# One decoder step on one core: low-rank steps placed one by one among a dense projection's groups, and a smaller rate of dense work in the second half

## Chip, core and metric

The kernel runs on one core of one Trainium2 chip. The metric is device time in microseconds, lower is better; a run's time is that of one execution of the whole step.

## What is computed

Two layers are applied to a prompt of 1024 tokens and to eight single sample tokens, width 1024, all in f32. Layer 0 is a convolution branch beside sparse attention. Layer 1, which the change touches, is an RWKV-7 mixer:

```python
xsh = x[None] + (x_prev - x)[None] * mu[:, None, None, :]
r, k, v, z = jnp.einsum('nbtd,nde->nbte', xsh[:4], w_rkvz)
w_raw = -jax.nn.softplus(-(w0 + jnp.tanh(xsh[4] @ w1) @ w2)) - 0.5      # "sigma"
decay = jnp.exp(-jnp.exp(w_raw))
a = jax.nn.sigmoid(a0 + (xsh[5] @ a1) @ a2)
...
def step(S, inp):          # one token
    sa = jnp.einsum('bhvk,bhk->bhv', S, kk_t)
    S = S * w_t[:, :, None, :] - sa[..., None] * (kk_t * a_t)[:, :, None, :] + v_t[..., None] * k_t[:, :, None, :]
    return S, jnp.einsum('bhvk,bhk->bhv', S, r_t)
...
out = (y.reshape(B, T, D_C) * jax.nn.silu(z)) @ w_out        # then x = layer_norm(ALPHA * x + out)
```

So there are four dense projections of 1024 x 1024 (r, k, v, z), two low-rank branches (rank 64), the recurrence, and one dense output product with a layer norm.

## The kernel before

The kernel runs layer 0 first and then layer 1 (`phase_d`, from about 1070 us on in the profile). Every f32 product is three passes of 32-bit "round" matmuls: each operand is split into a hi and a lo part, and hi x hi, lo x hi and hi x lo are summed (`mm3`, L1186 to L1188). A weight of 128 x 1024 comes in by DMA on SP's queue (`wsplit`, L1176); its hi part is made by ACT (L113) and its lo part by POOL or DVE (L121). It then feeds 48 matmuls for 512 tokens. The pool "dw" holds two each of the tiles `w`, `wh` and `wl`.

Each projection and branch is a Python generator, and who calls `next` on them in what order sets the order of emission; a scheduler then orders each engine's instructions by a simulated timeline. `xmake` makes a projection's mixed input (ACT L1209 and L1213, DVE L1210). `t_proj` yields twice for each weight (after each half of 256 tokens), evacuating by ACT L1321. `t_sigma` and `t_a` first run `lora_hidden`, then `lora_w2` makes the second matrix as A (hi, above lo's rows) and B, and then ten (sigma) or eight (a) small groups follow: matmuls L1278 and L1279 with L1281 and L1282 behind them, or L1296 and L1297 with L1298. `lora_w2` takes A and B from the names "wh" and "wl" of the same pool, and keeps them for all its groups.

Tokens come in two halves. The first half (`h` = 0, the "early" stage, about 1070 to 1270 us) follows the string `FSEQ`: k with sigma, then r with a, then v. After it come 16 units (`u`), one for each group of 128 tokens and half of the heads, with eight slots each. A slot does one step of the recurrence (`s3`), pieces of the preparation of the next units (`s2`, `joinUT`, `s1`), and then as much dense work from the list `F1` as `RATE` allows: generators yield their cost (1 unless they say otherwise). In units 0 to 5 F1 holds the second half's projections; what is left is run at the start of unit 6. From unit 6 on it holds z and the output products (`t_out`, L1703 to L1705 in `t_last` and L1774 to L1776), and each output reads the pairs of units that are done; `t_out(2)` is appended at unit 13 and `t_last` at unit 15. `t_out` takes two tiles "big" of a pool with two buffers, for the residual rows (L1757). Behind each output stands a layer norm, `ln_out` (ACT L1657, L1661, L1662; DVE L1667; POOL L1668). L1556 (ACT) is at the end of each unit's recurrence: unit ends stand at 1618 (unit 5), 1678, 1740, 1796, 1881, 1921 (unit 10), 1976, 2026 (unit 12), 2080, 2139 and 2175 us (unit 15: the program's tail begins).

Of the kernel before, what the change touches and what calls it, by code (L numbers as in the profile page):

```python
# [9 lines left out]
F32R = mybir.dt.float32r  # L10
# [719 lines left out]
WD = 3  # L730
SU = 1
TL = 1
RATE = 1.2, 1.1
WK1 = 5
SD = 0
CNAT = ('za', 0)
# [363 lines left out]
def phase_d(nc, tc, I, O, G):  # L1100
# [4 lines left out]
    flat = lambda t: t.rearrange("p a b -> p (a b)")  # L1105
    with ExitStack() as es:
        pool = lambda name, bufs, **k: es.enter_context(tc.tile_pool(name=name, bufs=bufs, **({} if k else {"reuse_waits": "tile"}), **k))
        B = (1, 2, 2, 9, 2, 3)
        up = pool("du", B[0])
        late = pool("dl", 1)  # L1110
        bp = pool("dbig", B[4])
# [4 lines left out]
        wp = pool("dw", B[2])  # L1116
# [135 lines left out]
        def lora_w2(nm):  # L1252
            w = flat(wtile())
            nc.sync.dma_start(w[0:64], I[nm + "2"])
            nc.sync.dma_start(w[64:128], I[nm + "2"])
            A = flat(wp.tile([128, 8, 128], F32R, name="wh"))
            nc.scalar.activation(A, w, AF.Copy)
            B = flat(wp.tile([128, 8, 128], F32R, name="wl"))
            nc.vector.tensor_tensor(B[0:64], w[0:64], A[0:64], op=SUB)
            v = flat(wtile())  # L1260
            nc.gpsimd.memset(v[64:128], 0.0)
            nc.sync.dma_start(v[64:65], I[nm + "0"])
            nc.sync.dma_start(v[96:97], I[nm + "0"])
            nc.scalar.activation(B[64:128], v[64:128], AF.Copy)
            nc.vector.tensor_tensor(B[96:97], v[96:97], B[96:97], op=SUB)
            return A, B

        def t_sigma(h):
            H1, H2 = lora_hidden(h, "w1", 4)
            yield  # L1270
            A, B = lora_w2("w")
            toks = [(i * 128, 128) for i in range(4)] + ([(512, NS)] if h else [])
            for ti, (o, r) in enumerate(toks):
                for c in range(2):
                    yield .3
                    p = acc()
                    sl = slice(c * 512, c * 512 + 512)
                    nc.tensor.matmul(p[0:r], lhsT=H1[:, o:o + r], rhs=A[:, sl], start=True, stop=False)  # L1278
                    nc.tensor.matmul(p[0:r], lhsT=H2[:, o:o + r], rhs=B[:, sl], start=False, stop=True)  # L1279
                    dst = otile()[:, 0:512]  # L1280
                    nc.scalar.activation(dst[0:r], p[0:r], AF.Tanh, scale=0.5)  # L1281
                    (nc.vector if "s" in EV else nc.gpsimd).tensor_scalar(dst[0:r], dst[0:r], 0.5, 0.5, op0=MUL, op1=ADD)  # L1282
                    nc.sync.dma_start(SG[4 * h + ti][:, sl] if ti < 4 else scr["sgs"][:, sl], dst[0:r])
            yield
# [19 lines left out]
        def t_proj(h, nm, i):  # L1304
            x = xmake(h, i)
            W = wsplit(I["w_rkvz"][i, 0])
            yield
            for j in range(8):
                wh, wl = W
                og = otile()  # L1310
                for c, g, lo, hi in chunks(h):
                    p = acc()
                    mm3(p[:, 0:hi - lo], wh, wl, x, lo, hi)
                    if c == 0 and j < 7:
                        W = wsplit(I["w_rkvz"][i, j + 1])
                    if nm == "z":
                        nc.scalar.activation(og[:, lo:hi], p[:, 0:hi - lo], AF.Tanh, scale=0.5)
                        nc.vector.scalar_tensor_tensor(og[:, lo:hi], og[:, lo:hi], 1.0, p[:, 0:hi - lo], op0=ADD, op1=MUL)
                        nc.sync.dma_start(SZ[g][:, j, 0:hi - lo], og[:, lo:hi])
                    else:  # L1320
                        nc.scalar.activation(og[:, lo:hi], p[:, 0:hi - lo], AF.Copy)  # L1321
                        if hi > 512:
                            nc.scalar.activation(smp[:, {"r": 0, "k": 1, "v": 2}[nm], j], p[:, 256:264], AF.Copy)
                    if c == 0:
                        yield
                if nm != "z":
                    nc.sync.dma_start(RT[nm, h, j // 4][:, j % 4], og[:, 0:512])
                yield
# [407 lines left out]
        def t_out(g):  # L1736
            n = 264 if g == 2 else 256
            y = xpair()
            for j in range(8):
                y[0].append(xp.tile([128, 264], F32R, name="xh"))  # L1740
                y[1].append(xp.tile([128, 264], F32R, name="xl"))
                og = sp.tile([128, 264], F32, name="og")
                nc.sync.dma_start(og[:, 0:256], YT[g][j // 4][:, j % 4])
                if g == 2:
                    nc.gpsimd.tensor_copy(og[:, 256:264], G.ysn[:, j])
                sz = sp.tile([128, 264], F32, name="xs")
                nc.sync.dma_start(sz[:, 0:256], SZ[g][:, j, 0:256])
                if g == 2:
                    nc.sync.dma_start(sz[:, 256:264], SZ[3][:, j, 256:264])
                nc.vector.scalar_tensor_tensor(sz[:, 0:n], og[:, 0:n], V(j, 4), sz[:, 0:n], op0=ADD, op1=MUL)  # L1750
                split(nc, y[0][j][:, 0:n], y[1][j][:, 0:n], sz[:, 0:n], nc.scalar, nc.vector, scale=0.5)
                if j % 2:
                    yield
            rows = [(0, 128), (128, 128)] + ([(256, NS)] if g == 2 else [])
            h = [bp.tile([128, D], F32, name="big") for _ in range(2)]
            for ti in range(2):
                nc.sync.dma_start(h[ti], scr["x1"][2 * g + ti])  # L1757
            H = [[x[:, 0:512], x[:, 512:]] for x in h]
            if g == 2:
                H.append([one.tile([128, 512], F32, name="xk", bufs=3) for _ in range(2)])  # L1760
                for f in range(2):
                    nc.sync.dma_start(H[2][f][0:NS], scr["x1"][8][0:NS, f * 512:f * 512 + 512])
            st = sp.tile([128, 3, 8], F32, name="st")
            for f in range(2):
                fs = slice(f * 512, f * 512 + 512)
                p = [(ps if ti < 2 else pm).tile([128, 512], F32, name="mm" if ti < 2 else "sm") for ti in range(len(rows))]
                for k2 in range(4):
                    wh, wl = wsplit(I["w_out1"][f, k2])
                    for k in range(2):
                        a, b = (w[:, 4 * k:4 * k + 4].rearrange("p a b -> p (a b)") for w in (wh, wl))  # L1770
                        kk = 2 * k2 + k
                        for ti, (o, r) in enumerate(rows):
                            yh, yl = y[0][kk][:, o:o + r], y[1][kk][:, o:o + r]
                            nc.tensor.matmul(p[ti][0:r], lhsT=yh, rhs=a, start=kk == 0, stop=False)  # L1774
                            nc.tensor.matmul(p[ti][0:r], lhsT=yh, rhs=b, start=False, stop=False)  # L1775
                            nc.tensor.matmul(p[ti][0:r], lhsT=yl, rhs=a, start=False, stop=kk == 7)  # L1776
                    yield
                for ti, (o, r) in enumerate(rows):
                    nc.vector.scalar_tensor_tensor(H[ti][f][0:r], H[ti][f][0:r], ALPHA, p[ti][0:r],
                                                   op0=MUL, op1=ADD, accum_out=st[0:r, ti, f:f + 1])  # L1780
            gb = []
            for i in (1, 3):
                gb.append(flat(wtile()))
                nc.sync.dma_start(gb[-1], I["ln_rows"][i:i + 1].to_broadcast([128, D]))
            parts = [[(h[ti], slice(0, D))] if ti < 2 else [(H[2][f], slice(f * 512, f * 512 + 512)) for f in range(2)]
                     for ti in range(len(rows))]
            ln_out(rows, parts, st, gb, g, [nc.vector if g == 3 and ti else nc.gpsimd for ti in range(len(rows))])
            yield

        def run(gens, cost):  # L1790
            while gens and cost > 0:
                try:
                    cost -= next(gens[0]) or 1.0
                except StopIteration:
                    gens.pop(0)
            return -cost
# [23 lines left out]
        for g in (g1[0], g1[1], g2[0], gj[0]):  # L1820
            for _ in g:
                pass
        F1 = [t_proj(1, "k", 1), t_sigma(1), t_proj(1, "r", 0), t_a(1), t_proj(1, "v", 2)]
        F3 = []
        over = 0.0
        for u, (g, d) in enumerate(units):
            if u == 6:
                run(F1, 1000)
                F1 = [t_proj(0, "z", 3), t_out(0), t_proj(1, "z", 3), t_out(1)]
# [6 lines left out]
            for k in range(8):  # L1836
# [5 lines left out]
                step(g1[u + 2])  # L1842
                over = run(F1, RATE[u >= 6] - over)
                if k in (2, 6) and u < 11:
# [136 lines left out]
```

## Time and profile before

| what | us |
|---|---|
| median of three runs | 2218.49 |
| the three | 2222.84, 2218.19, 2218.49 |
| the profiled execution, its own time | 2221.96 |
| its span in the trace | 2220.2 |
| busy in it: PE, DVE, ACT, POOL | 1849.8, 1494.3, 1156.8, 979.1 |
| mean granted TensorE clock | 0.867 of full speed |

The span runs from the first to the last instruction; the time has 1.8 us more around it. The granted clock is the share of full speed that the chip's throttle allowed TensorE. Waits are named by what ended them: "ACT wh L113 <- PE mm L1187" means that the split on line 113 could begin when the matmuls of line 1187 had read the old tile.

### The profile page before, as it was taken

The page shows a single profiled execution, that of the slowest core. Times are in us where ns is not written, and L with a number is a line of the kernel's source. Part 1 is how long each engine was busy: PE and PEld are TensorE (multiplying, and loading weights), DVE is VectorE, ACT ScalarE, POOL GpSimd, SP SyncE. Part 2 cuts the span into 40 slices and gives each one's busy share as a digit, 9 for nine tenths or more (in the row PEclk, how much of TensorE's full clock was granted, in tenths as well). Part 3 has the DMA queues.
Part 4 walks back from the last instruction along what each step waited for, and adds up shares of the span by engine and source line. Part 5 has one row for each costly group of instructions (what it writes and reads, how often), then busy time and mean ns, then how long its engine had stood idle before and what let it go on. Part 6 is the DMA issues. An engine that isn't in the chain of part 4 may idle for free. (4 is left out here: it accounts for less than half of the span.)

```text
span 2220.2 us, 41377 instructions
## 1 busy us (share of the span) xinstructions
PE 1849.8 (83%) x16026; PEld 1552.5 (70%) x16026; DVE 1494.3 (67%) x2543; ACT 1156.8 (52%) x2361; POOL 979.1 (44%) x784
## 2 busy tenths in 40 slices
PE   5988897668999997898777999899999786987854
PEld 5987896656767785676666987687788665865533
DVE  5998995547788878226363276856747896487553
ACT  3323323544665545357466465847754585465344
POOL 4667666544655545545334212332344444113233
PEclk9998998857999976899887999897799885987967
DMA  6423344521221213636455443433443454353432
GB/s 241 128 84 131 135 143 152 200 71 34 63 62 47 57 34 96 201 118 184 143 183 183 149 115 102 150 114 109 144 145 118 147 148 136 91 143 113 133 111 102
DMA packets 232095, 275.27 MB, mean 124 GB/s; under 512 B 71545, under 2 KB 171569, under 8 KB 227738
## 3 DMA queue, kind: packets, MB, share of 16 engines
q1 hardware_dynamic: 210712, 215.21, 31.8%
q0 software_dynamic: 7616, 41.52, 5.6%
q10 hardware_dynamic: 13570, 15.90, 2.0%
q8 instruction: 126, 2.06, 0.4%
q14 instruction: 71, 0.58, 0.1%
HBM read 212.47 MB, written 64.27 MB: 125 GB/s over the span
## 5 line engine op out<-in xcount | busy, mean ns | idle before, releaser
L121 POOL TENSOR_TENSOR wl<-w,wh 128x1024 fp32r<-128x1024 f32 x81 | 201.5, 2489 | 353.7 <-ACT wh L113 317.9
L1186 PE MATMUL mm<-xh,wh 128*128 128x256 f32 (+1 forms) x1024 | 310.8, 305 | 17.6 <-ACT og L1321 6.6
L1187 PE MATMUL mm<-xl,wh 128*128 128x256 f32 (+1 forms) x1024 | 302.4, 296 | 1.2 <-POOL xl L1214 0.7
L1188 PE MATMUL mm<-xh,wl 128*128 128x256 f32 (+1 forms) x1024 | 300.4, 295 | 3.5 <-POOL wl L121 2.7
L113 ACT ACTIVATE wh<-w 128x1024 fp32r<-128x1024 f32 (+2 forms) x130 | 134.4, 1035 | 191.6 <-DMA w<-in_w_fm 60.9
L1186 PEld LDWEIGHTS mm<-xh,wh 128*128 128x128 f32 x1024 | 204.3, 200 | 30.0 <-ACT og L1321 9.1
L1187 PEld LDWEIGHTS mm<-xl,wh 128*128 128x128 f32 x1024 | 205.8, 201 | 5.7 <-issue 2.7
L1188 PEld LDWEIGHTS mm<-xh,wl 128*128 128x128 f32 x1024 | 204.3, 200 | 6.2 <-POOL wl L121 3.4
L268 DVE SCALAR_TENSOR_TENSOR c<-U,cw,c 128x1024 f32<-128x1024 f32 x120 | 199.1, 1683 | 0.9
L604 POOL TENSOR_TENSOR Pl<-PT,Ph 128x512 fp32r<-128x512 f32 (+1 forms) x102 | 131.9, 1297 | 151.3 <-DVE Ph L603 121.0
L252 POOL TENSOR_TENSOR cbuf<-cbuf 128x256 f32<-128x256 f32 (+2 forms) x72 | 132.8, 1850 | 87.6 <-ACT cbuf L250 83.5
L217 PE MATMUL S<-xh,wh 128*128 128x344 f32 (+1 forms) x432 | 146.6, 339 | 22.8 <-ACT wh L113 20.4
L219 PE MATMUL S<-xh,wl 128*128 128x344 f32 (+1 forms) x432 | 144.8, 335 | 15.6 <-POOL wl L121 12.3
L218 PE MATMUL S<-xl,wh 128*128 128x344 f32 (+1 forms) x432 | 146.4, 339 | 4.1 <-POOL xl L121 3.9
L1214 POOL TENSOR_TENSOR xl<-xs,xh 128x520 fp32r<-128x520 f32 (+1 forms) x76 | 106.0, 1398 | 98.8 <-ACT xh L1213 91.2
L250 ACT ACTIVATE cbuf<-cbuf,wrow 128x256 f32<-128x256 f32 x192 | 79.3, 496 | 120.3 <-DMA cbuf<-in_ccmp,cix 77.3
L1210 DVE SCALAR_TENSOR_TENSOR xs<-xk,mu,xs 128x512 f32<-128x512 f32 x96 | 97.1, 1017 | 56.9 <-ACT xs L1209 55.1
L217 PEld LDWEIGHTS S<-xh,wh 128*128 128x128 f32 (+1 forms) x432 | 84.8, 196 | 25.0 <-ACT wh L113 23.6
L562 DVE TENSOR_REDUCE nm<-S 128x1 f32<-128x640 f32 (+7 forms) x128 | 88.0, 698 | 19.8 <-PE S L558 19.1
L219 PEld LDWEIGHTS S<-xh,wl 128*128 128x128 f32 (+1 forms) x432 | 84.3, 195 | 20.6 <-POOL wl L121 14.4
L1398 PE MATMUL pa<-AM,KBK 64*128 64x128 f32 x512 | 70.5, 327 | 29.3 <-DVE KBK L1376 13.2
L218 PEld LDWEIGHTS S<-xl,wh 128*128 128x128 f32 (+1 forms) x432 | 84.8, 196 | 7.7 <-POOL xl L121 4.8
(610 smaller groups left out, 5396.8 us busy)
## 6 DMA issues: line engine op xcount, KB each, us to landing
w<-in_w_rkvz SPq DMA_DIRECT2D x64, 512.0 KB
w<-in_w_out SPq DMA_DIRECT2D x36, 512.0 KB
w<-in_w_fm SPq DMA_DIRECT2D x25, 512.0 KB
xk<-x1T SPq DMA_DIRECT2D x48, 260.0 KB
xk<-x1T SPq DMA_DIRECT2D x48, 256.0 KB
w<-in_w_out SPq DMA_DIRECT2D x16, 256.0 KB
x<-in_xp SPq DMA_DIRECT2D x8, 512.0 KB
x<-x ACTq DMA_DIRECT2D x8, 512.0 KB
```

The costliest lines, as they stand in the source:

```text
L113: nc.scalar.activation(hi, src, AF.Copy, **({} if scale is None else {"scale": scale}))
L121: e_lo.tensor_tensor(lo, src, hi, op=SUB)
L217: nc.tensor.matmul(dst, lhsT=wh[:, k, 0:n], rhs=xh[:, k, sl], start=k == 0, stop=False)
L218: nc.tensor.matmul(dst, lhsT=wh[:, k, 0:n], rhs=xl[:, k, sl], start=False, stop=False)
L219: nc.tensor.matmul(dst, lhsT=wl[:, k, 0:n], rhs=xh[:, k, sl], start=False, stop=k == 7)
L252: nc.gpsimd.tensor_tensor(bv[:, 0:n], bv[:, 0:n], bv[:, n:2 * n], op=ADD)
L268: e.scalar_tensor_tensor(c[:, i, 0:T], u[:, k:k + T], cwh[:, i, k:k + 1], c[:, i, 0:T], op0=MUL, op1=ADD)
L604: lambda: nc.gpsimd.tensor_tensor(Pl[:, 0:w], PT[:, 0:w], Ph[:, 0:w], op=SUB)]
L1186: nc.tensor.matmul(dst, lhsT=wh[:, k], rhs=xh[k][:, lo:hi], start=k == 0, stop=False)
L1187: nc.tensor.matmul(dst, lhsT=wh[:, k], rhs=xl[k][:, lo:hi], start=False, stop=False)
L1188: nc.tensor.matmul(dst, lhsT=wl[:, k], rhs=xh[k][:, lo:hi], start=False, stop=k == 7)
L1214: (nc.vector if early[0] and k % LD == 0 else nc.gpsimd).tensor_tensor(lo[k][:, 0:n], t[:, 0:n], hi[k][:, 0:n], op=SUB)
```

## The change

There are four edits. The second matrix of a low-rank branch, A and B, is taken from the pool of "big" and no longer from "wh" and "wl". In the second half's list F1 the branches are no longer generators of their own between the projections: a new generator `among` emits sigma's groups one by one between the half-weight groups of r, and a's between those of v; each such pair counts 1.15. The four preparation steps of `t_out` count 0.25 and not 1. From unit six on, `RATE` is 0.9 and no longer 1.1 per slot. The early stage's string is untouched.

```diff
-RATE = 1.2, 1.1
+RATE = 1.2, 0.9
...
-            A = flat(wp.tile([128, 8, 128], F32R, name="wh"))
+            A = flat(bp.tile([128, 8, 128], F32R, name="big"))
             nc.scalar.activation(A, w, AF.Copy)
-            B = flat(wp.tile([128, 8, 128], F32R, name="wl"))
+            B = flat(bp.tile([128, 8, 128], F32R, name="big"))
...
                 if j % 2:
-                    yield
+                    yield .25
...
+        def among(proj, lora):
+            yield next(lora) or 1.5
+            yield next(proj)
+            next(lora)
+            for _ in proj:
+                next(lora, None)
+                yield 1.15
+            for x in lora:
+                yield x
...
-        F1 = [t_proj(1, "k", 1), t_sigma(1), t_proj(1, "r", 0), t_a(1), t_proj(1, "v", 2)]
+        F1 = [t_proj(1, "k", 1), among(t_proj(1, "r", 0), t_sigma(1)), among(t_proj(1, "v", 2), t_a(1))]
```

The first place is ACT in the early stage, r beside a (names end in a running number; `og_10390` and `og_10460` are results of r, `og_10450` and `og_10520` of a, `xs` and `xh` an input being made for later). Before:

```order
L1209 ACTIVATE xs_11755<-xk_11756,omu_9080 128x520
L1321 ACTIVATE og_10460<-mm_10461 128x256
L1209 ACTIVATE xs_11766<-xk_11767,omu_9080 128x520
L1213 ACTIVATE xh_11753<-xs_11755 128x520
L113 ACTIVATE wh_10488<-w_10486 128x1024
L1321 ACTIVATE og_10460<-mm_10493 128x256
L1298 ACTIVATE og_10520<-mm_10521 128x256
```

With the change:

```order
L1321 ACTIVATE og_10390<-mm_10423 128x256
L1298 ACTIVATE og_10450<-mm_10451 128x256
L113 ACTIVATE wh_10488<-w_10486 128x1024
L1209 ACTIVATE xs_10756<-xk_10757,omu_9080 128x512
L1213 ACTIVATE xh_10744<-xs_10746 128x512
L1298 ACTIVATE og_10450<-mm_10455 128x256
L1213 ACTIVATE xh_10754<-xs_10756 128x512
L1321 ACTIVATE og_10460<-mm_10461 128x256
L1209 ACTIVATE xs_10766<-xk_10767,omu_9080 128x512
L1209 ACTIVATE xs_10776<-xk_10777,omu_9080 128x512
L1213 ACTIVATE xh_10764<-xs_10766 128x512
```

The split `wh_10488` of the next r weight stood behind `og_10460<-mm_10461`, the evacuation of the weight in use; it now stands ahead of it and of three input steps. `wh_10558` follows in the same way.

The second place is SP's queue in the early stage, k beside sigma (`w_9651`, `w_9718` and `w_9785` are k's first weights, `xk` pieces of x, `rk00` and `rk01` results of k that are stored, `kt` unit 0's load of them). Before:

```order
L1327 DMA rk00_9103<-og_9552 128x512
L1204 DMA xk_9958<-x1T_0_80 128x512
L1176 DMA w_9651<-in_w_rkvz 128x1024
L1204 DMA xk_9968<-x1T_0_80 128x512
L1176 DMA w_9718<-in_w_rkvz 128x1024
L1327 DMA rk01_9104<-og_9625 128x512
L1095 DMA x1T_1_81<-xt_9007 1024x1x8
L1176 DMA w_9785<-in_w_rkvz 128x1024
L1283 DMA sg0_9119<-og_9688 128x512
L1336 DMA kt_11270<-rk00_9103 128x4x128
```

With the change:

```order
L1327 DMA rk00_9103<-og_9552 128x512
L1263 DMA w_9619<-in_w0 1x1024
L1204 DMA xk_9958<-x1T_0_80 128x512
L1204 DMA xk_9968<-x1T_0_80 128x512
L1327 DMA rk01_9104<-og_9625 128x512
L1095 DMA x1T_1_81<-xt_9007 1024x1x8
L1336 DMA kt_11270<-rk00_9103 128x4x128
L1176 DMA w_9651<-in_w_rkvz 128x1024
L1176 DMA w_9718<-in_w_rkvz 128x1024
L1283 DMA sg0_9119<-og_9688 128x512
L1338 DMA st__11273<-sg0_9119 128x512
L1176 DMA w_9785<-in_w_rkvz 128x1024
```

The two weights stood ahead of the store of `og_9625` and the x1T store; they now stand behind both, and behind unit 0's load `kt`. The two residual loads of `t_out(0)` (L1757) are no longer in this place.

The third place is ACT from the end of unit 15 (L1556) on (`wh` are splits of output weights, `xh` inputs of the last output). Before:

```order
L1556 ACTIVATE sq_22500<-pA_22498 128x512
L1558 ACTIVATE Y_22147<-pA_22498,vec_9084 128x128 x4
L1562 ACT_TABLE_LOAD
L1562 ACTIVATE sq_22500<-pB_22506,eps_gn_66 128x512
L1563 ACT_TABLE_LOAD
L1563 ACTIVATE sq_22500<-sq_22500 128x512
L113 ACTIVATE wh_22389<-w_22387 128x1024
L113 ACTIVATE wh_22534<-w_22532 128x1024
L113 ACTIVATE xh_22174<-xs_22512 128x128
L113 ACTIVATE xh_22175<-xs_22517 128x128
```

With the change:

```order
L1556 ACTIVATE sq_22500<-pA_22498 128x512
L1558 ACTIVATE Y_22147<-pA_22498,vec_9084 128x128 x4
L113 ACTIVATE wh_22382<-w_22380 128x1024
L1562 ACT_TABLE_LOAD
L1562 ACTIVATE sq_22500<-pB_22506,eps_gn_66 128x512
L1563 ACT_TABLE_LOAD
L1563 ACTIVATE sq_22500<-sq_22500 128x512
L113 ACTIVATE wh_22394<-w_22392 128x1024
L113 ACTIVATE xh_22174<-xs_22512 128x128
L113 ACTIVATE xh_22175<-xs_22517 128x128
L113 ACTIVATE wh_22428<-w_22426 128x1024
L113 ACTIVATE xh_22176<-xs_22522 128x128
```

Between L1556 and `wh_22534`, the first weight of the last tile's second part, there was one weight split, and now there are four.

Counted on PE between the unit ends in the two orders, dense matmuls of z and of the outputs (behind unit 12 all are of the outputs):

| | unit 8 | 9 | 10 | 11 | 12 | 13 | 14 | 15 | behind it |
|---|---|---|---|---|---|---|---|---|---|
| before | 90 | 102 | 216 | 144 | 72 | 72 | 72 | 55 | 41 |
| with the change | 120 | 72 | 168 | 168 | 96 | 48 | 144 | 24 | 72 |

## Rows read from the trace of the kernel before

**Rows 1.** Part 1 of the page: busy time, share of the span and instructions of PE; then of PEld, DVE and the others.
```profile
PE 1849.8 (83%) x16026; PEld 1552.5 (70%) x16026; DVE 1494.3 (67%) x2543; ACT 1156.8 (52%) x2361; POOL 979.1 (44%) x784
```

**Rows 2.** Busy time of each engine by stretch: stretch in us from the span's start, its length, then busy us (instructions) of PE, PEld, DVE, ACT and POOL, the granted TensorE clock as a share of full speed, the busy share of the DMA engines and their GB/s. The first two are k beside sigma and r beside a in the early stage, the third the dense v projection there, the rest units 2, 3, 6, 9, 10, 14 and 15, what follows unit 15, and all from the end of unit 12.
```profile
1077.80:1108.20 30.40, 23.89 (x149) 21.94 (x150) 6.46 (x5) 7.93 (x18) 6.85 (x6) 0.83 0.50 166
1166.90:1197.40 30.50, 25.55 (x156) 24.17 (x156) 8.97 (x12) 13.32 (x27) 12.71 (x13) 0.79 0.52 176
1232.00:1263.00 31.00, 31.00 (x266) 31.00 (x265) 5.03 (x6) 10.30 (x20) 7.76 (x4) 1.00 0.44 149
1402.00:1448.00 46.00, 41.33 (x473) 30.53 (x473) 42.22 (x81) 41.26 (x86) 19.16 (x22) 0.81 0.51 155
1448.00:1500.00 52.00, 51.41 (x645) 46.60 (x644) 26.39 (x57) 21.86 (x49) 13.48 (x12) 1.00 0.40 122
1618.00:1678.00 60.00, 60.00 (x719) 53.18 (x718) 25.07 (x42) 32.06 (x64) 21.81 (x17) 1.00 0.41 132
1796.00:1881.00 85.00, 58.42 (x756) 46.24 (x755) 70.09 (x133) 53.73 (x105) 38.54 (x32) 0.70 0.48 148
1881.00:1921.00 40.00, 40.00 (x526) 35.85 (x525) 12.25 (x27) 15.08 (x30) 10.85 (x7) 1.00 0.33 104
2080.00:2139.00 59.00, 37.85 (x516) 25.60 (x514) 36.80 (x75) 25.08 (x54) 20.33 (x10) 0.77 0.21 59
2139.00:2175.00 36.00, 30.30 (x260) 20.75 (x260) 11.81 (x27) 16.98 (x30) 9.52 (x5) 0.81 0.61 199
2175.00:2221.00 46.00, 17.29 (x43) 11.29 (x43) 18.72 (x34) 19.48 (x30) 14.94 (x6) 0.67 0.24 83
2026.00:2221.00 195.00, 126.52 (x1242) 85.51 (x1241) 107.62 (x207) 83.21 (x155) 66.12 (x34) 0.75 0.37 119
```

**Rows 3.** Waits of all engines between 1040 and 1260 us: engine, tile and line that waited, for which, us in total, times, longest.
```profile
POOL wl L121 <- ACT wh L113: 59.0, 10, 9.9
ACT wh L113 <- PE mm L1187: 15.3, 7, 2.3
```

**Rows 4.** Timeline of PE: start, duration (us), line, operation, and in brackets the idle time before it and what ended it. The first seven rows are r beside a, from the last matmul before the first stall to the last of the third weight, with two neighbours (1172.41, 1172.62) behind a stall; the last two are from k beside sigma.
```profile
1162.79 0.38 PE L1297 MATMUL mm<-xl,wl 128*128 128x256 f32 x1
1166.87 0.58 PE L1296 MATMUL mm<-xh,wh 128*128 128x256 f32 x1 [3.70 <-ACT og L1321]
1172.41 0.41 PE L1188 MATMUL mm<-xh,wl 128*128 128x256 f32 x1
1172.62 0.41 PE L1186 MATMUL mm<-xh,wh 128*128 128x256 f32 x1
1178.72 0.39 PE L1296 MATMUL mm<-xh,wh 128*128 128x256 f32 x1 [2.10 <-ACT og L1321]
1188.44 0.39 PE L1296 MATMUL mm<-xh,wh 128*128 128x256 f32 x1 [1.06 <-ACT og L1321]
1197.32 0.28 PE L1297 MATMUL mm<-xl,wl 128*128 128x256 f32 x1
...
1077.82 0.39 PE L1186 MATMUL mm<-xh,wh 128*128 128x256 f32 x1 [1.19 <-ACT wh L113]
1084.59 0.40 PE L1279 MATMUL mm<-wl,xl 128*128 128x512 f32 x1
```

**Rows 5.** The load of the weight that is split at 1165.49: its issue on SP's queue, and on ACT its hi part.
```profile
1160.24 0.33 SPq L1176 DMA_DIRECT2D w<-in_w_rkvz  x1
...
1165.49 1.06 ACT L113 ACTIVATE wh<-w 128x1024 fp32r<-128x1024 f32 x1 [2.41 <-DMA w<-in_w_rkvz]
```

**Rows 6.** k beside sigma: issues on SP's queue (the first two k weights, and unit 0's load of kt), the hi part of the first k weight on ACT, and on DVE the last instruction that reads a buffer that one of those weights takes.
```profile
1072.62 0.33 SPq L1176 DMA_DIRECT2D w<-in_w_rkvz  x1
1074.53 0.33 SPq L1176 DMA_DIRECT2D w<-in_w_rkvz  x1
1080.57 0.58 SPq L1336 DMA_DIRECT2D kt<-rk  x1
...
1076.71 1.06 ACT L113 ACTIVATE wh<-w 128x1024 fp32r<-128x1024 f32 x1 [0.35 <-DMA w<-in_w_rkvz]
...
1073.28 1.22 DVE L1265 TENSOR_TENSOR wl<-w,wl 1x1024 fp32r<-1x1024 f32 x1
```

**Rows 7.** ACT in the last 195 us: the last hi part before, and the first behind, a stretch without any; then three of the last output's. And two neighbouring output matmuls of the tail on PE.
```profile
2093.94 1.06 ACT L113 ACTIVATE wh<-w 128x1024 fp32r<-128x1024 f32 x1 [2.30 <-issue]
2147.22 1.06 ACT L113 ACTIVATE wh<-w 128x1024 fp32r<-128x1024 f32 x1 [0.99 <-DMA w<-in_w_out]
...
2190.41 1.04 ACT L113 ACTIVATE wh<-w 128x1024 fp32r<-128x1024 f32 x1
2194.79 1.04 ACT L113 ACTIVATE wh<-w 128x1024 fp32r<-128x1024 f32 x1
2198.89 1.06 ACT L113 ACTIVATE wh<-w 128x1024 fp32r<-128x1024 f32 x1 [3.07 <-PE pa L1705]
...
2171.92 0.40 PE L1703 MATMUL mm<-wh,xh 128*128 128x512 f32 x1
2172.15 0.40 PE L1704 MATMUL mm<-wl,xh 128*128 128x512 f32 x1
```

**Rows 8.** The layer norm's rows at 2122 us: L1667 on DVE by itself and beside POOL's L1668.
```profile
2121.68 0.81 DVE L1667 TENSOR_SCALAR big<-big,st 128x1024 f32<-128x1024 f32 x1
2122.61 2.86 DVE L1667 TENSOR_SCALAR big<-big,st 128x1024 f32<-128x1024 f32 x1
...
2122.57 2.35 POOL L1668 TENSOR_TENSOR big<-big,w 128x1024 f32<-128x1024 f32 x1 [24.39 <-DVE big L1667]
```

**Rows 9.** Waits of PE between 1800 and 1880 us, the longest: us in total, times, longest.
```profile
PE pA L1523 <- DVE SV L1549: 11.7, 1, 11.7
```

## Prediction, made before the changed kernel ran

> **What bounds the kernel now.** I read the busy shares first: PE works for 83% of the span, more than any other engine [rows 1]. That is an average, so the table of stretches comes next [rows 2]; there the reader is to see three kinds of stretch. In the dense v projection of the early stage (1232 to 1263) PE is busy for all 31.0 us, 266 matmuls, 0.117 us each. In units 6 (1618 to 1678) and 10 (1881 to 1921) PE is also busy throughout. Elsewhere it is not: in the two early stretches where a low-rank branch runs beside a dense projection (1077.8 to 1108.2 and 1166.9 to 1197.4) it is busy for 23.9 of 30.4 and 25.6 of 30.5 us at a granted clock of about 0.8; in units 2, 9 and 14 DVE or a chain of small steps is ahead of it.
>
> The two early stretches are explained by the waits of that stage [rows 3]: POOL's lo part (L121) waited 59.0 us for ACT's hi part (L113), and L113 waited 15.3 us for PE's L1187, the last reader of the old weight. The second low-rank matrix A holds one of the two "wh" buffers for the whole branch, so the next weight can be split only when PE has finished the last. The PE timeline shows what that costs at a weight's start [rows 4]: gaps of 3.70 and 2.10 us, then matmuls 0.21 us apart (1172.41, 1172.62), twice the dense pitch: the clock's lower level, 1.2 instead of 2.4 GHz.
>
> **The change part by part.** Every sum is made against the profiled execution (2221.96 us, 0.16% above the median of the three, 2218.49) and then taken off the median.
>
> *The bp buffers, r with a (early).* A no longer holds a "wh", so a weight is split while its predecessor is in use. From the last matmul before the first stall (1162.79) to the end of the third weight (1197.32) pass 34.5 us [rows 4]. Without the stalls a weight costs 48 x 0.118 = 5.7 us plus a seam of 1.3 us (the gap of 1.19 us at 1077.82, behind which the stretch started at full clock), 7.0 in all; three of them and 12 low-rank matmuls (1.4) are 22.4. The load must come earlier too: w was issued at 1160.24 and its split waited for it until 1165.49 [rows 5]; in the new order ACT has that split ahead of three input steps, not behind a projection's evacuation. **-12.1 us.** Ends: 0 (the stalls only change their cause) and -16 (dense pitch, 3 x 5.7 + 1.4 = 18.5).
>
> *The same, k with sigma (early).* Here the new order costs something first. SP issued the first two k weights at 1072.62 and 1074.53 [rows 6]; they now stand behind the load of kt, which was issued at 1080.57. First matmul before: 1077.82. Now: about 1080.3, plus 4.1 us of transfer (1072.62 to the split's start at 1076.71) and 1.06 of split, 1085.5: 7.7 us later. Queued behind the late weights is nothing that PE needs sooner. The three weights then take 3 x 7.0 = 21.0 in place of 30.4, 9.4 less. **-1.7 us.** Ends: -9.4 (the loads come no later, since their buffers come free by DVE's L1265 at 1074.5) and +7.7 (the stalls stay).
>
> *Units 0 to 5.* k, r, v, sigma and a of the second half are the same work; sigma's ten groups move from unit 2 (DVE 42.2 and ACT 41.3 of 46 us) into unit 3, where PE has 51.4 of 52. That relieves one and loads the other by 20 matmuls of 0.40 = 8.0 us (the last row there) [rows 4]. I price it at **0**, ends -8 and +8. The big buffers that the two matrices now take in units 2 to 5 hold nothing else there: t_out(0), which shares them, needs its two residual tiles, now loaded later, only for its first sum in unit 8.
>
> *RATE 0.9 and 0.25 a preparation step (units 6 to 15).* By cost, z and out are now spread over 54/0.9 = 60 slots instead of 60/1.1 = 54.5. Counted in the two orders, 288 output matmuls stand behind the end of unit 12 on PE where 240 stood. The 48 take 48 x 0.235 = 11.3 us (the pitch of L1703 to L1704) [rows 7]. They leave units 6 to 12, 408 us (1618 to 2026), of which 100 (units 6 and 10) are bound by PE: 11.3 x 100/408 = **-2.8 us** gained. They come to the last 195 us, in which PE is idle for 68, so I let that cover hide them; without that cover they cost 11.3. Ends: -11.3 (all of them were in the way) and +17 (unit 14 pays for its whole 72).
>
> *The sum:* -12.1 - 1.7 + 0 - 2.8 = -16.6: 2205.4 against the profiled run, **2202 us** against the median.
>
> **The rivals.** A measurement of this kernel can tell about 0.2% (4.4 us) from no change.
>
> *The late pile-up (slower).* Unit 14 (2080 to 2139) gets 144 output matmuls instead of 72: 16.9 us more of PE. Behind the last unit 72 matmuls of the last output stand instead of 41, three more weights, whose splits came 4.1 to 4.4 us apart [rows 7]: 7.3 us of PE at least, 12.6 by the splits. That is 24 to 29.5 if none of it is hidden, and given back would be at most what units 13 and 15 lose, 24 and 31 matmuls, 12.9. So 11 to 29.5 late, less the 13.8 early: 2216 to 2234, about 2228 if little is given back. It decides when the recurrence's small matmuls, on which unit 14's steps hang, must queue on PE behind the outputs, and when the stretch behind unit 15 is paced by weights. For it: units 13 and 15 end by their own chains, so less work there need not shorten them, and in the last stretch (2175 to 2221) the splits are spaced out already. Against: unit 14 has PE busy for 37.9 of 59 us [rows 2], 21.1 idle, and from 2093.94 to 2147.22 no output weight was split at all [rows 7]: its room is larger than the 16.9. Its upper end has a second reason: DVE's L1667 took 0.81 us by itself and 2.86 beside POOL's L1668 of 2.35 us [rows 8]; with three layer norm tiles pushed together, 2.05 each is up to 6 us more of the same sign. The Trainium skill ("SBUF — State Buffer", Who interferes with whom) says that VectorE and GpSimd share a port pair that is an exclusive lock; the pair of rows agrees in that DVE's end falls with POOL's, and by it the pile-up would come to the upper end that it has here.
>
> *Unit 9 too (faster still).* It takes 85 us where PE has 58.4 and DVE 70.1 of work [rows 2], with one PE wait of 11.7 us for DVE's SV at L1549 [rows 9]. In the new order it has 72 dense matmuls and not 102. If its steps fall out of each other's way, it comes to between DVE's 70.1 and PE's 58.4: 15 to 27 less, 2175 to 2187, about 2181. Against: this wait is on the recurrence's own chain, which the change leaves alone.
>
> *No gain early.* If PE still pauses at each weight long enough, the lower clock stays: 48 x 0.213 + 1.3 = 11.5 us a weight, three are 34.5, as long as now. Then only the late -2.8 is left: about 2216. For it: the granted clock of 0.79 in that stretch [rows 2], and loads that could pace it (each weight 4.1 us or more after its issue). Against: the 1.19 us gap at 1077.82, after which the matmul took 0.39 and not 0.58 us [rows 4]. The Trainium skill ("TensorE: Matmul & The Clock Gate", Part 1: The HAM clock gate) has the clock follow how busy PE has lately been; by that rule shorter gaps bring the full clock, and the sum would be that of the forecast, while by the row of 1166.87 alone (0.58 us after its gap) it would be this rival.
>
> **How the numbers follow.** Forecast 0.50 (its own range 2192 to 2212: r with a off by 4, the other three terms by 6 together); unit 9 too 0.17; late pile-up 0.20; no gain early 0.13. Faster by over 0.2%: 0.50 + 0.17 + 0.03 of the last = 0.70. Within: 0.10 of the last and 0.02 of the pile-up = 0.12. Slower: 0.18. The range reaches from 2178 (half of unit 9's case lies below) to 2229 (half of the pile-up's case lies above), so some 0.18 is left out.
>
> **What would show it.** Early: no gap above 1.5 us at a weight's start while a runs beside r, three weights in 21 to 24 us, a granted clock near 1.0 there; the first k weight at 1085 rather than 1078. If k starts at 1078 the gain is larger by up to 7.7; if a's stretch keeps its 30 us, the no-gain case holds. Units 6 to 12: 408 us becomes about 405; if unit 9 falls to 70 us or below, its case. Late: from the end of unit 12 to the end about 195 us; 205 or more is the pile-up. The prediction is wrong if the time before unit 0 does not fall by 10 us or more, or if the last stretch grows by as much.

## Result: 1.06% longer, and the profile after

The changed kernel took 2237.59 us (median of four, 2236.02 to 2239.89) where the kernel before, in runs beside it, took 2218.34 (four, 2213.85 to 2222.84): ratio 1.0106, 95% interval 1.0078 to 1.0135. The forecast was 2202 us; the time is above the range's end of 2229 as well. The rival that came nearest is the late pile-up (2216 to 2234).

Part 1 of the page of the changed kernel answers to [rows 1]:

```profile
PE 1861.1 (83%) x16026; PEld 1558.5 (70%) x16026; DVE 1495.5 (67%) x2543; ACT 1148.6 (51%) x2355; POOL 979.1 (44%) x784
```

PE is 11.3 us busier with the same 16026 instructions, and the span is 2234.3 us, 14.1 longer. To see where the time went, I set the two traces on the first projection's first matmul (1004.5 before, 999.2 after: the two runs differ by 5.3 us ahead of any change) and compared the unit ends (start of L1556 on ACT). Negative is earlier with the change:

| end of | early stage and unit 0 | 1 | 2 | 4 | 5 | 6 | 7 | 8 | 9 | 10 | 12 | 13 | 14 | 15 | program |
|---|---|---|---|---|---|---|---|---|---|---|---|---|---|---|---|
| us | -10 | 0 | -2 | -5 | -32 | -9 | 8 | 16 | -4 | 8 | 1 | -5 | -5 | 14 | 19 |

So 10 us are won early and given back in unit 1 (48 us long instead of 38); dense work leaves unit 5 and comes back in units 6 to 8; unit 9 is 20 us shorter; by unit 12 the traces are level, and all of the loss appears behind unit 14. The stretches of the changed kernel, with the columns of [rows 2]: k beside sigma (from k's fifth weight to r's first), r beside a (from r's second weight to v's first), the middle of the latter, units 5, 6 and 7, units 14 and 15, what follows, and all behind unit 12:

```profile
1063.60:1116.40 52.80, 34.83 (x217) 29.73 (x215) 20.86 (x21) 23.88 (x46) 18.48 (x22) 0.81 0.54 170
1124.00:1199.80 75.80, 55.84 (x403) 52.59 (x403) 39.20 (x49) 48.75 (x94) 37.30 (x41) 0.88 0.63 199
1159.00:1189.00 30.00, 21.71 (x169) 20.27 (x167) 13.90 (x18) 18.58 (x37) 17.52 (x17) 0.99 0.70 217
1546.00:1580.00 34.00, 30.42 (x257) 23.37 (x257) 26.91 (x60) 21.09 (x44) 12.02 (x17) 0.65 0.36 92
1580.00:1663.00 83.00, 74.36 (x929) 67.05 (x929) 30.86 (x56) 46.92 (x111) 22.57 (x20) 0.96 0.46 146
1663.00:1743.00 80.00, 68.74 (x771) 58.56 (x770) 61.83 (x104) 36.20 (x74) 32.49 (x29) 0.87 0.40 121
2069.00:2129.00 60.00, 53.54 (x445) 32.43 (x444) 25.43 (x58) 20.63 (x34) 15.75 (x9) 0.88 0.46 149
2129.00:2183.00 54.00, 27.06 (x269) 19.76 (x270) 29.51 (x54) 18.74 (x42) 20.06 (x10) 0.62 0.40 121
2183.00:2234.00 51.00, 23.15 (x67) 14.90 (x65) 19.11 (x35) 23.26 (x34) 20.04 (x8) 0.72 0.30 103
2022.00:2234.00 212.00, 144.65 (x1330) 99.20 (x1328) 110.37 (x222) 88.44 (x166) 71.91 (x40) 0.76 0.38 119
```

The kernel before took 53.8 and 82.7 us for the first two of these (same columns):

```profile
1068.70:1122.50 53.80, 36.50 (x217) 30.68 (x215) 21.20 (x21) 24.88 (x48) 17.73 (x22) 0.80 0.55 178
1131.00:1213.70 82.70, 61.54 (x405) 57.05 (x403) 37.42 (x48) 48.31 (x92) 35.72 (x40) 0.82 0.55 176
```

Behind unit 12 it is 212 us instead of 195. Unit 14 keeps its length with 144 output matmuls (PE 53.5 of 60 us busy, 37.9 of 59 before), so its idle time did take them; unit 15 takes 54 us instead of 36, and what follows 51 instead of 45.

### The profile page after: what moved, and what is told of

The parts are those of the page before. It is cut to its first block, busy times and chain, and to the rows that moved or that the text cites. A ratio compares the mean times of both kernels' runs of the same rounds, so it can differ in the third digit from the quotient of the medians.

```text
span 2234.3 us, 41381 instructions
## 1 busy us (share of the span) xinstructions
PE 1861.1 (83%) x16026; PEld 1558.5 (70%) x16026; DVE 1495.5 (67%) x2543; ACT 1148.6 (51%) x2355; POOL 979.1 (44%) x784
## 5 line engine op out<-in xcount | busy, mean ns | idle before, releaser
L121 POOL TENSOR_TENSOR wl<-w,wh 128x1024 fp32r<-128x1024 f32 x81 | 202.4, 2499 | 345.3 <-ACT wh L113 328.6
L113 ACT ACTIVATE wh<-w 128x1024 fp32r<-128x1024 f32 (+2 forms) x130 | 134.5, 1035 | 206.9 <-PE mm L1187 59.1
L121 DVE TENSOR_TENSOR wl<-w,wh 128x1024 fp32r<-128x1024 f32 x45 | 57.0, 1266 | 54.6 <-ACT wh L113 54.3
```

Source lines behind the costliest of these rows:

```text
L113: nc.scalar.activation(hi, src, AF.Copy, **({} if scale is None else {"scale": scale}))
L121: e_lo.tensor_tensor(lo, src, hi, op=SUB)
```

## Experiments

Each ratio is to runs of the kernel before on the same chip; the brackets are 95% intervals. Single runs of one kernel spread far: 33 runs of the kernel before, taken side by side, lay between 2195.95 and 2222.30 us. So terms of 5 us are barely resolved even by a dozen runs.

### The parts of the change, one by one

`e1_early_big`: A and B in big in the early stage alone.

```diff
-            A = flat(wp.tile([128, 8, 128], F32R, name="wh"))
+            A = flat((bp if early[0] else wp).tile([128, 8, 128], F32R, name="big" if early[0] else "wh"))
...
-            B = flat(wp.tile([128, 8, 128], F32R, name="wl"))
+            B = flat((bp if early[0] else wp).tile([128, 8, 128], F32R, name="big" if early[0] else "wl"))
```

> The kernel before, with A and B of the early stage's two branches alone taken from the pool of big (the second half's stay in wh and wl; F1, yields and RATE as before). Theory L (the buffers gain early, the late rate loses): the early stage ends about 10 us sooner and the end follows, 2208 us. Theory M (the groups among r and v lose it): the same, 2208. Rival N (time won early is lost again in the units whatever else is changed): 2218, unit 0 about 10 us sooner and unit 12 not.

`e2_big`: A and B in big in both halves, as in the change, nothing else.

> The kernel before, with A and B of both halves taken from the pool of big, nothing else. L and M: 2208 us, as with the early half alone or a few us less, since units 2 to 5 lose their weight stalls too. Rival N: 2218 or more, the residual tiles of the first output wait for a's last group.

`e3_big_among`: that, and the new F1 with `among`.

> Both buffer changes and the new list F1 with its groups among r and v; RATE stays 1.1 from unit six on and a preparation step counts 1. L: 2208 us, since the groups among the weights cost nothing. M: the first weight of r and of v waits for its branch, v's weights are left for units 6 and 7, about 20 more than with the buffers alone: 2228.

`e4_rate_yield`: the kernel before with the change's other two edits.

```diff
-RATE = 1.2, 1.1
+RATE = 1.2, 0.9
...
-                    yield
+                    yield .25
```

> The kernel before with RATE 0.9 from unit six on and 0.25 for a preparation step, nothing else. L: late pile-up, from the end of unit 12 to the end 212 us in place of 195, 2218 + 18 = 2236 us or above. M: within 5 us of the kernel before, 2218.

Measured:

| kernel | median, us | ratio |
|---|---|---|
| e1_early_big | 2209.53 | 0.9983 [0.9955, 1.0011] |
| e2_big | 2207.62 | 0.9982 [0.9955, 1.0009] |
| e3_big_among | 2209.66 | 0.9993 [0.9959, 1.0026] |
| e4_rate_yield | 2223.83 | 1.0071 [1.0035, 1.0107] |

The kernel before was at 2213.49 beside these. The buffers gain 4 us at best guess and no more than 10, and both intervals take in no gain at all, so that the times do not rule out rival N; in the trace of e2 the early gain (11 us at unit 0's end) is still there at the end (10 us). The groups among the weights cost 0.0011 more than the buffers alone, nothing that can be measured, so theory M's 2228 us fell. The rate with the 0.25 costs 16 us (8 to 24) without the rest: theory L had the right part, with too large a number (2236 or above).

### The rate and the 0.25 apart

`e5_after_rate11` is the changed kernel with `RATE = 1.2, 1.1`; `e6_rate_only` and `e7_yield_only` are the kernel before with one line of e4's diff each. `e8_after_drain` is the changed kernel with

```diff
-                over = run(F1, RATE[u >= 6] - over)
+                over = run(F1, (2.0 if u >= 13 else RATE[u >= 6]) - over)
```

> The change with RATE 1.1 from unit six on as before; the buffers, the new F1 and the 0.25 stay. Theory T (the end follows the last matmul of output 2 by a fixed 108 to 115 us of layer norm, preparation and last weights, and the smaller rate moves that matmul): output 2 costs 10 and not 13 and starts at unit 13 as before, so its last matmul comes no later than in the kernel before, 110 us before the end, and the time is 2213 us or up to 10 less. Rival M (the groups among r and v lose it): 2230, as v's weights still fall into unit 6.

> The kernel before with RATE 0.9 from unit six on and nothing else (a preparation step counts 1). T: output 2 is finished only behind unit 15, its last matmul 20 us or more later than with 0.25, and the time is 2240 to 2260 us, worse than the rate and the 0.25 together (2224). Rival P (the 0.25 does the harm, because it bunches an output's matmuls): 2215.

> The kernel before with 0.25 for a preparation step and nothing else. T: output 2 is done some slots sooner, 2200 to 2213 us. Rival P: 2224 or more.

> The change with 0.9 up to unit 12 and 2.0 from unit 13 on, so that all is as in the changed kernel until then and output 2 is fed out faster. T: the last matmul of output 2 comes about 20 us sooner and the end with it, about 2215 us. Rival Q (units 13 to 15 have no room for the work that 0.9 leaves to them, in whatever order): 2235 or more.

Measured: e5 2233.32 us, 1.0077 [1.0046, 1.0108]; e6 2232.36, 1.0069 [1.0042, 1.0096]; e7 2227.97, 1.0072 [1.0050, 1.0094]; e8 2239.54, 1.0102 [1.0068, 1.0136]. The kernel before: 2212.96. Theory T, one chain from output 2 alone, missed all four (e6 in size only), and M's number for e5 fits by accident, since e3 has the same groups and loses nothing. Rival P has e7's number and not e6's, rival Q has e8's. The 0.25 by itself loses 15 us where it should gain, the rate by itself loses 15, and both together lose no more than either. The traces show that the two lose in opposite places. Of e6, unit 15 and what follows it; of e7, unit 13 and what follows unit 15:

```profile
2102.00:2145.00 43.00, 34.67 (x278) 21.81 (x276) 13.17 (x39) 21.11 (x36) 7.14 (x3) 0.94 0.25 82
2145.00:2237.00 92.00, 36.59 (x98) 23.56 (x98) 41.08 (x65) 30.62 (x49) 41.08 (x18) 0.61 0.36 118
```

```profile
2035.00:2101.00 66.00, 53.91 (x498) 34.58 (x499) 31.20 (x68) 27.63 (x51) 15.71 (x9) 0.88 0.23 73
2184.00:2221.00 37.00, 12.28 (x29) 7.82 (x27) 15.28 (x31) 14.78 (x26) 11.72 (x5) 0.65 0.21 74
```

With the smaller rate the recurrence is through early, 23 us before the same point of the kernel before when the starts are aligned, and then 92 us follow in place of 45: all 96 matmuls of the last output stand behind unit 15. With the 0.25 the outputs' matmuls come in bursts, 133 of them in unit 13, which takes 66 us and not 54; the recurrence ends 16 us late, and only 37 us follow. That gave theory C, two ends: output 2's last matmul plus a tail of 103 to 115 us, and unit 15's end plus 37 to 45 us. In the kernel before 115 and 45 us follow the two points (2105 and 2175), both at the upper bound of their range; I took that for a balance, in which a move to either side makes the other one late. This is a reading: each tail is counted back from the same end, so that the two sums agree in any kernel. e8 fits it: fed at 2.0 the outputs delay unit 15 to 2198, and 45 us follow, while output 2's last matmul, at 2133, comes no sooner than in the changed kernel.

### What makes the tail behind output 2

The tail from output 2's last matmul to the end was 115 us before, 110 after the change, 108 in e4 and 103 in e6. `e15_prep_early_09`, `e16_prep_early_09_y` and `e17_after_prep_early` (RATE 0.9; that with 0.25; the changed kernel) take the last output's first eight preparations out of it:

```diff
             for j in range(8):
                 prep(j, 0, None)
+                yield
...
+            if u == 14:
+                gl = t_last()
             if u == 15:
-                F1.append(t_last())
+                F1.append(gl)
...
+                if u == 14:
+                    step(gl)
                 over = run(F1, RATE[u >= 6] - over)
```

and pack `y` of `t_out` and `t_last` two to a 520-wide tile, so that both outputs' inputs fit.

> The kernel before with RATE 0.9 (2232 us with nothing else), and with the last output's first eight preparation steps issued one per slot in unit 14, ahead of output 2's end; for that the outputs' inputs are packed two to a buffer. Theory C (two chains end the kernel: output 2's last matmul plus 103 to 115 us of layer norm, preparation and last weights, and unit 15's end plus 37 to 45; a smaller rate makes the first one late): the first eight preparations took 28 us of the first chain, 2232 - 28 = 2204 us. Rival W (that chain is paced by the loads of the output weights, the preparation is beside them): 2232.

> The same with 0.25 for a preparation step of the earlier outputs (2224 us without the early preparation). C: both chains, 2110 + 80 and 2158 + 45, end near 2203 us in the place of 2224. W: 2224.

> The changed kernel with the same early preparation. C: output 2's last matmul at 2124 plus 80 is no longer last; unit 15's end at 2183 plus 45 is: 2228 us in place of 2237. W: 2237.

Measured: e15 2246.29 us, 1.0182 [1.0139, 1.0225]; e16 2227.90, 1.0067 [1.0028, 1.0106]; e17 2231.82, 1.0085 [1.0053, 1.0118]; before 2211.79. Theory C's numbers for e15 and e16 fell, by 42 and 25 us; W's for e16 came close, and e17 lies between the two. e15 is slower even than e6: its output 2 ends 20 us later (1155 and 1136 us behind the first projection matmul), with the same tail, and why is open. In e16 and e17 seven of the eight preparations did run 22 to 44 us ahead of output 2's last matmul, and the tail behind it kept 104 and 105 us. So it did not hang on these eight. The weights' queue showed another hold. In the kernel before, SP's issues of output 2's layer norm rows and of the next output weight, and POOL's last instruction that reads those rows:

```profile
2092.58 0.36 SPq L1784 DMA_DIRECT2D w<-in_ln_rows  x1
2100.34 0.59 SPq L1784 DMA_DIRECT2D w<-in_ln_rows  x1
...
2136.20 2.57 POOL L1669 TENSOR_TENSOR xk<-xk,w 8x512 f32<-8x512 f32 x2
...
2143.15 0.38 SPq L1176 DMA_DIRECT2D w<-in_w_out  x1
```

In the changed kernel:

```profile
2112.63 0.33 SPq L1784 DMA_DIRECT2D w<-in_ln_rows  x1
...
2154.71 2.56 POOL L1669 TENSOR_TENSOR xk<-xk,w 8x512 f32<-8x512 f32 x2
...
2163.32 0.37 SPq L1176 DMA_DIRECT2D w<-in_w_out  x1
```

The gain and bias rows sit in `w`, in both weight buffers, from before output 2's last matmul until its layer norm has read them. The last output's first weight can be issued only then: 38 us behind that matmul in both (2105.3 to 2143.2, 2124.8 to 2163.3). That is the stretch without a split [rows 7], which the prediction took for spare room. Four kernels put the rows of output 2 elsewhere:

```diff
-                gb.append(flat(wtile()))
+                gb.append(flat(wtile()) if g != 2 else (up if i == 1 else us).tile(
+                    [128, 1536], F32, name="KBK" if i == 1 else "AM", bufs=B[0] if i == 1 else B[5])[:, 0:D])
```

> The kernel before; for output 2 alone the layer norm's gain and bias rows go into two tiles that the finished units have left (KBK and AM) and no longer into the two weight buffers w. Theory R (the stretch from output 2's last matmul to the end, 103 to 115 us in all kernels but those whose unit 13 takes most of it, is so long because its layer norm holds both weight buffers until L1669, so the last output's first weight is issued some 38 us behind that matmul): weights of the last output are split between 2094 and 2147, that stretch falls by 20 or more, and the end is then set by unit 15, 2175 + 37 to 45: 2212 us or up to 8 less. Rival S (the preparation of the last output's inputs gates it, not its weights): 2212, and the stretch still 105 to 115.

> The changed kernel with output 2's rows in those two tiles. R: the last matmul of output 2 at 2124 plus some 85 us is no longer last, unit 15's end at 2183 plus 37 to 45 is: 2220 to 2228 us in place of 2238. S: 2238.

> The kernel before with RATE 0.9 and 0.25, and output 2's rows in those two tiles. R: 2224 less 15 to 20, 2205 us, since its unit 15 ends 60 us before the end. S: 2224.

> RATE 0.9, 0.25, the early preparation of the last output's inputs, and output 2's rows in those two tiles: both of the things that could stand between output 2 and the last output are taken away. R and S: 2228 less 20 to 30, about 2203 us. Rival V (what follows output 2 is bound by neither, but by the last units' own steps): 2224 to 2228.

Measured, with the kernel before at 2213.53: e18 2205.81 us, 0.9968 [0.9946, 0.9990]; e19 2232.32, 1.0078 [1.0050, 1.0107]; e20 2225.43, 1.0043 [1.0009, 1.0076]; e22 2221.92, 1.0041 [1.0021, 1.0061]. In e18, on PE: output 2's last matmul, the last output's first, its last ones before a stop, and the one behind the stop; then on SP and DVE the store of unit 14's result, its loads, and the input made of it:

```profile
2098.15 0.40 PE L1776 MATMUL sm<-wh,xl 128*8 128x512 f32 x1
...
2110.97 0.74 PE L1703 MATMUL mm<-wh,xh 128*128 128x512 f32 x1
...
2113.97 0.73 PE L1705 MATMUL mm<-wh,xl 128*128 128x512 f32 x2
...
2148.22 0.51 PE L1703 MATMUL sm<-wh,xh 128*128 128x512 f32 x1 [1.84 <-ACT xh L113]
...
2142.10 0.55 SPq L1569 DMA_DIRECT2D yt<-sq  x1
2145.51 3.13 SPq L1681 DMA_DIRECT2D og<-yt  x4
...
2147.47 0.35 DVE L1682 SCALAR_TENSOR_TENSOR xs<-og,vec,xs 128x128 f32<-128x128 f32 x1 [2.86 <-DMA og<-yt]
```

Between the first two lie 13 us, where 44 lay before (2105 to 2149). So the rows did hold the first weight. But the tail did not hang on that: only 12 of the last output's 96 matmuls move ahead, and the thirteenth waits until 2148.2, 50 us behind output 2's last matmul, where it was 52 before (2105.3 to 2157.4). It waits for an input's split (ACT xh L113), not for a weight. That input belongs to the last output's second tile, which is made from unit 14's result: the unit ends at 2135.0, its result is stored at 2142.1 and loaded from 2145.5 on. e15 to e17 had moved the first tile's preparation alone. So the stretch without a split [rows 7] is still there in e18 (2098.6 to 2151.9), and the tail is 113 us.

Neither theory holds as it was priced. R has e18's time, but not the 20 us off the stretch; S has the stretch (105 to 115) and e20's time, but not e18's gain; e19 lies between them, and e22 is nearest to V. Only e18's own interval shows a gain, of 0.3%; e19 to the change and e20 to e4 give the same quotient with intervals that overlap. What e18's 7 us are is open: set on the first projection matmul, its trace keeps within 0.6 us of the kernel before at every unit end up to unit 13, and ends 1.8 us sooner.

Last, two kernels with what had not lost: `e25_big_rows` (A and B in big, output 2's rows as in e18) and `e26_big_rows_rate10`, the same with `RATE = 1.2, 1.0`.

> The kernel before with the two things that did not lose: A and B of both halves in big, and output 2's layer norm rows in the tiles of finished units. If both add up (0.9982 and 0.9968): 0.995 of the kernel before, about 2202 us. If the one end is behind the other (unit 15's end plus 45): 0.997 to 0.998.

> The same with RATE 1.0 from unit six on. Theory C (with output 2's tail shortened, unit 15's end is last, and a slower feed lets the units end sooner): 0.990 to 0.995 of the kernel before. Rival V (any move of the feed away from 1.1 loses, for the units' own steps collide with another output's): 1.000 or above.

Measured: e25 2207.54 us, 0.9972 [0.9947, 0.9998]; e26 2199.47, 0.9946 [0.9919, 0.9972]; before 2214.02. By the ratio e26 is 12 us below the kernel before, and well below the changed one; C's range holds it, V's does not. But the mechanism is not C's: unit 15 ends some 31 us sooner, when the starts are aligned, and then 60 us follow, not 37 to 45. The intervals of e25 and e26 overlap, so that the rate by itself gains there is likely, not shown. RATE 1.0 on the kernel before with nothing else, and any rate above 1.1, were not tried.

### r beside a

`e10_og_own` is e1 with `KO = "ksrv"` and `OG2 = 2`: a's results get output buffers of their own in the early stage.

> The early-buffer kernel (A and B of the early stage in big) with an output pool of its own, two buffers, for a's groups in the early stage, so that r's results no longer share the two og buffers with a's. Theory G (r beside a is now held by the og buffers: PE waited 12.6 us for L1321 and L1298, and these for the stores): r beside a, from r's first weight to v's first, falls from 76.7 us by 5 to 10, the time from about 2209 to 2202. Rival (the loads of the weights or of a's input pace it): 76 us, 2209.

Measured: 2207.62 us, 0.9981 [0.9958, 1.0004], as e1, and r beside a took 77.3 us. G fell. The waits of the first matmul of a's groups, by group of PE's instructions, in the stretch of r beside a: before, with the change, and in e10 (busy us and mean ns; idle before, by releaser):

```profile
L1296 PE MATMUL mm<-xh,wh 128*128 128x256 f32 x16 | 6.8, 428 | 15.4 <-ACT og L1321 8.6 <-ACT og L1298 6.8
```

```profile
L1296 PE MATMUL mm<-xh,big 128*128 128x256 f32 x16 | 6.4, 404 | 12.6 <-ACT og L1321 7.1 <-ACT og L1298 5.4
```

```profile
L1296 PE MATMUL mm<-xh,big 128*128 128x256 f32 x16 | 6.7, 419 | 11.9 <-ACT og L1321 6.3 <-ACT og L1298 5.6
```

PE waits for the evacuations L1321 and L1298 in all three. Each a group needs both PSUM buffers "mm" right after r's groups used them, and ACT evacuates between input steps. More PSUM buffers for a were not tried.

## Why the prediction was wrong, step by step

- **k beside sigma (-1.7): right in sum.** 53.8 us became 52.8. The weight that the prediction calls the first, k's sixth, came later as worked out: 9.1 us behind the stretch's start before (1077.8 - 1068.7), 16.4 with the change (1080.0 - 1063.6), 7.3 later where 7.7 was forecast. The three weights took 23.6 us, not 21.0.
- **r beside a (-12.1): the size nearly right where it was priced, the mechanism in part.** From the last matmul before the first stall to the end of the third weight the changed kernel takes 24.4 us (the first and third line below) where 34.5 passed before [rows 4], 10.1 less. Nine traces with the old early text have 30.9 to 34.7 there, eleven with the early buffers 24.3 to 26.5.

```profile
1159.46 0.28 PE L1297 MATMUL mm<-xl,big 128*128 128x256 f32 x1
1169.66 0.38 PE L1296 MATMUL mm<-xh,big 128*128 128x256 f32 x1 [2.78 <-ACT og L1321]
1183.88 0.28 PE L1297 MATMUL mm<-xl,big 128*128 128x256 f32 x1
...
1145.24 0.58 PE L1186 MATMUL mm<-xh,wh 128*128 128x256 f32 x1 [4.28 <-DVE xs L1244]
```

Most of this is the clock: it was granted in full (0.99 between 1159 and 1189, against 0.79 in the like stretch before [rows 2]), and a weight's 48 matmuls took 5.9 us instead of 8.1 to 8.8. The Trainium skill ("TensorE: Matmul & The Clock Gate", Part 1: The HAM clock gate) has the clock follow PE's recent work. This agrees with the row. But the gaps did not all go: 3.70, 2.10 and 1.06 us became 2.78 and 1.55, so that "no gap above 1.5 us" failed. The rows on which the term stood name ACT og L1321 as their releaser [rows 4], not a weight split, and I read them as weight stalls since L113 and L121 waited as well [rows 3]. Of the 15.4 us of waits at L1296 12.6 are left. And 3.7 us go again ahead of the priced stretch, where PE now waits 4.28 us for a's hidden layer (L1244): from r's second weight to v's first 82.7 us became 75.8, 6.9 less. From the first projection matmul to v's first matmul the traces take 209.2 and 200.6 us, 8.6 less where the two early terms are 13.8. In whole runs the buffers gave 4 us (e1, e2), with intervals that take in 0.
- **Units 0 to 5 (0): right in the runs, not in the traces.** v's weights moved from unit 5 into units 6 and 7 (units 5 to 7 took 61, 60 and 62 us before, and 34, 83 and 80), and e3 stands within 0.0011 of e2. But unit 1 takes 46 to 48 us in all six traces with the new list and 34 to 39 in the other fourteen. So the list costs some 10 us there, and it is open how much of that comes back.
- **The rate and the 0.25 (-2.8): wrong, and this is the step that decided.** They cost 16 us (e4), near the bound of +17. I spread the gain over time in which PE is busy and hid the cost in time in which it is idle, as if PE's capacity were the limit behind unit 12. It is not: PE was idle for 68 of 195 us there before [rows 2] and still is for 67 of 212; that stretch grew by 17, the prediction's own sign of being wrong. The work hangs on chains of latency: either edit alone loses 15 us, the rate behind unit 15 (e6: 92 us instead of 45), the 0.25 ahead of it (e7: unit 15 ends 16 us late). In the changed kernel, counted from the first projection matmul, output 2's last matmul comes 25 us later than before and unit 15's end 14 us later.
- **The late rival** was right in sign, place and nearly in size, and wrong in its detail: unit 14 did not grow (60 us for 59). What grew is unit 15, into which output 2's layer norm slid. DVE there, and POOL's L1668 and L1669, in the changed kernel; then the longest of PE's waits in unit 15:

```profile
2139.13 0.80 DVE L1667 TENSOR_SCALAR big<-big,st 128x1024 f32<-128x1024 f32 x1
2140.57 2.83 DVE L1667 TENSOR_SCALAR big<-big,st 128x1024 f32<-128x1024 f32 x1
2146.05 2.70 DVE L1565 TENSOR_TENSOR sq<-sq,bv 128x512 f32<-128x512 f32 x1
2190.55 0.69 DVE L1565 TENSOR_TENSOR sq<-sq,bv 128x512 f32<-128x512 f32 x1
...
2140.01 2.83 POOL L1668 TENSOR_TENSOR big<-big,w 128x1024 f32<-128x1024 f32 x1 [21.51 <-DVE big L1667]
2145.81 2.38 POOL L1669 TENSOR_TENSOR big<-big,w 128x1024 f32<-128x1024 f32 x1
```

```profile
PE pA L1523 <- DVE UT L1513: 9.6, 1, 9.6
```

The recurrence's own L1565 takes 2.70 us beside POOL's work and 0.69 by itself, and a step of the recurrence (L1523) waits 9.6 us for DVE behind this. The Trainium skill ("SBUF — State Buffer", Who interferes with whom) has the two engines share a port pair that is an exclusive lock. The two times of L1565 agree with it. That the slide of the layer norm, and not something else in unit 15, makes its 18 us is argued from these rows; no kernel moved the layer norm alone.
- **Unit 9** fell from 85 to 64 us, as that rival had it, and in e7 to 67; yet the time came back in units 10 to 13 of e7 (20 us more in unit 10, 16 in unit 12, 12 in unit 13) and at the end of the changed kernel. A stall that goes is no gain when the end hangs elsewhere.

Still open: the parts add up to about +14 us (e2 -4, e3 against e2 +2, e4 +16), the change measured +23 (17 to 30). The intervals nearly meet; what the rest would be is not settled, and the 10 us of unit 1 may be part of it. That the rate and the 0.25 make most of the loss is shown by e3 and e4. Why they do is read from traces: the two ends of theory C are argued, its numbers missed in e15 and e16, and no kernel took the wait for unit 14's result away.

## What to carry to other kernels

When the releaser of a gap is named in the row, price the gap on that releaser, not on another wait of the same stretch. Idle time of an engine is not room for work that waits on something else: behind the last bulk work ask which chains end the kernel, and what each step of them waits for. Here a slower feed (0.9) and a burstier one (0.25) both lost, in opposite places. A stretch in which a stream stands still is not spare room until it is known what holds the stream; and when one hold is taken away, ask what the stream waits for next, for two can lie behind each other, as the rows and unit 14's result do here.

## Not expected of the hardware

Executions of one kernel spread by 1.2% here (2195.95 to 2222.30 us in 33), and much of that can lie ahead of the first changed instruction (the first projection matmul stands at 989 to 1007 us in the twenty traces). After a gap of 2.28 us the first k matmul of the changed kernel took 0.58 us, where it took 0.39 after 1.19 us before [rows 4].
